# Seven products for the first column group too, one sum of weights added by DMA, and buffers granted by late times, in a two-layer encoder on one core

## The chip, the cores and the metric

The kernel runs on one core of a Trainium2 chip, as one program with one launch. The metric is the device time of one execution in microseconds. TensorE (PE) multiplies, VectorE (DVE) and ScalarE (ACT) prepare its operands and read its results, GpSimd (POOL) issues some transfers and does small work, SyncE (SP) issues the other transfers.

## The reference

The reference is a trunk of two layers on 512 tokens of width 1024, in float32. Each layer has a SwiGLU feed-forward, a mixer (layer 0: global and windowed attention; layer 1: neighbourhood attention), attention into 256 memory tokens, and a second SwiGLU feed-forward, each with a residual sum and a LayerNorm. The change is in the feed-forwards, of which there are four (0 to 3, each with its own weights):

```python
def swiglu(x, w_gate, w_up, w_down):            # 1024 -> 2816 -> 1024
    return (jax.nn.silu(x @ w_gate) * (x @ w_up)) @ w_down

y = swiglu(x, ffn_w_gate[i, 0], ffn_w_up[i, 0], ffn_w_down[i, 0])
x = layer_norm(ALPHA * x + 0.5 * y, ln_g[i, 0], ln_b[i, 0])
```

## The kernel before

**Numbers.** A float32 operand is split into a high part (a cast to fp32r, on ACT) and a low part (the difference, on DVE), and a product is three matmuls: high by high, high by low, low by high (`mm3`, line 334). `wide` (line 340) makes both parts of a weight tile of 128 x 1024 elements. For the tiles named in `ADDED` (only the fourth) the low part is made by a transfer that POOL issues and that adds the raw weights onto their negated high part in SBUF.

**The feed-forward** works on groups of 256 of the 2816 columns. `hidden` (line 585) computes gate and up of one group for all tokens. It cuts the work into quarters (the 1024 rows of the weights in two halves, gate and up as the other side; the tokens in two halves) and forms them from seven products of quarters with sums, in place of eight products. A product is 2 x 4 x 3 = 24 matmuls of 256 columns; `self.right[m]` is the tokens' side of product m, and `left[m]` the weights' side. The weights' side needs four sums, s1 to s4, each a DVE instruction over 128 x 1024 elements, then a high and a low part for each of seven tiles; s1 is up's first half plus up's second half, and s2 to s4 follow from it or from the raw weights:

```python
s1 = self.mix(new(), w["21"], w["22"], ALU.add)
s2 = self.mix(new(), s1, w["11"], ALU.subtract)
```

The tokens' side of products 5, 6, 7 and 4 (t1 to t4) is made by `mixed_features` (line 430) from the raw quarters of the features, once a feed-forward; products 1, 2 and 3 take plain quarters. The first group of each feed-forward does not use this: `ffn_by_tokens` (line 520) goes through the four tiles of 128 tokens and needs for each the features of this tile alone: 2 x 8 x 3 = 24 matmuls for gate and 24 for up, four times, so 192 matmuls of 256 columns, and then 8 transposes of 128 x 128 that turn the result back to the layout of `hidden`. `mixed_features` stands behind it. So a feed-forward is one group by tokens and ten by `hidden`, with the products into the output (`down_fast`, `down`) between them; the three groups at its end are those of `TAIL`.

**Between two stages** the LayerNorm goes by token tiles t = 0 to 3 (`finish`, line 727): DVE and ACT compute it, POOL raises one number a token to the power -0.5, then PE turns the tile to features (`to_features`, line 405: two times four transposes), ACT casts the high part (`xh`), DVE makes the low part (`xl`), and ACT copies the raw quarter for `mixed_features` (`keep`).

**The order of the work** is set by a planner, `Graph.emit` (line 178). Every operation is first recorded (all of them have line 153 in the profile, so tiles tell them apart). The planner then plays the program through with a cost for each operation: each engine takes, of what is ready, the operation that is earliest in program order, and the instructions are written out in that order, one in-order stream for each engine. An operation is ready when its operands are and when its tiles have a buffer. Buffers are shared by tag (35 of 4 KB a partition for `slab`, 5 PSUM banks for `u`, 3 for `d`), and are granted in the order in which the program asks for the tiles.

## Time and profile before

| | |
|---|---|
| median of 3 runs (lowest, highest) | 2147.81 us (2146.98, 2147.91) |
| the profiled execution: its time, its span | 2146.15 us, 2144.4 us |
| granted TensorE clock, mean | 0.999 of full speed |
| PE busy | 2123.5 us (99%), 14212 matmuls |
| weight loads (PEld) busy | 1959.1 us (91%) |
| DVE, ACT, POOL busy | 1701.1 us (79%), 1123.1 us (52%), 243.2 us (11%) |
| transfers | 261.41 MB, mean 122 GB/s |

The time is the device's for the whole execution; the span goes from the first to the last instruction, so the profiled execution has 1.75 us around its span. Of the table PE's row matters most: where PE is idle is where something else sets the time.

### The profile page before, as it was taken

The page shows a single profiled execution, that of the slowest core. Times are in us where ns is not written, and L with a number is a line of the kernel's source. Part 1 is how long each engine was busy: PE and PEld are TensorE (multiplying, and loading weights), DVE is VectorE, ACT ScalarE, POOL GpSimd, SP SyncE. Part 2 cuts the span into 40 slices and gives each one's busy share as a digit, 9 for nine tenths or more (in the row PEclk, how much of TensorE's full clock was granted, in tenths as well). Part 3 has the DMA queues.
Part 4 walks back from the last instruction along what each step waited for, and adds up shares of the span by engine and source line. Part 5 has one row for each costly group of instructions (what it writes and reads, how often), then busy time and mean ns, then how long its engine had stood idle before and what let it go on. Part 6 is the DMA issues. An engine that isn't in the chain of part 4 may idle for free.

```text
span 2144.4 us, 35357 instructions
## 1 busy us (share of the span) xinstructions
PE 2123.5 (99%) x14212; PEld 1959.1 (91%) x14212; DVE 1701.1 (79%) x2405; ACT 1123.1 (52%) x1722; POOL 243.2 (11%) x379
## 2 busy tenths in 40 slices
PE   9999999999999999999999999999999999999998
PEld 9989898778998898989999998999989989989897
DVE  7998976688855899889798989766678458998995
ACT  6555555467533564645464554545554435656452
POOL 0000004544000000000000000023320000000000
PEclk9999999999999999999999999999999999999999
DMA  7344358113433253435343525436455332434352
GB/s 207 99 138 129 118 148 208 20 40 89 151 103 112 89 157 109 129 108 148 108 116 111 148 89 158 148 84 162 134 185 154 99 109 79 129 108 137 102 152 62
DMA packets 186516, 261.41 MB, mean 122 GB/s; under 512 B 10864, under 2 KB 141552, under 8 KB 186352
## 3 DMA queue, kind: packets, MB, share of 16 engines
q1 hardware_dynamic: 175792, 221.40, 33.9%
q0 software_dynamic: 10560, 37.75, 8.3%
q8 instruction: 111, 1.82, 0.4%
q14 instruction: 53, 0.43, 0.1%
HBM read 217.17 MB, written 4.19 MB: 103 GB/s over the span
## 4 chain that ended last, share of the span: by engine, by line
PE 96%; DVE 1%; ACT 1%; issue 1%; POOL 0%; SPq 0%; DMA 0%; POOLq 0%; DVEq 0%; ACTq 0%
PE u L153 67%; PE d L153 29%; DVE slab L153 1%; ACT slab L153 0%; ACT t L153 0%; DVE x L153 0%; DVE mn L153 0%; DVE t L153 0%; ACT xh L153 0%; SPq L153 0%; ACT L153 0%; DMA slab<-t 0%; POOL slab L153 0%; POOL lny L153 0%; DVE l L153 0%
## 5 line engine op out<-in xcount | busy, mean ns | idle before, releaser
L153 DVE TENSOR_TENSOR slab<-slab,slab 128x1024 fp32r<-128x1024 f32 (+2 forms) x808 | 933.6, 1190 | 44.3 <-ACT slab L153 36.6
L153 ACT CAST slab<-slab 128x1024 fp32r<-128x1024 f32 (+1 forms) x620 | 608.6, 1016 | 194.1 <-DVE slab L153 155.1
L153 PE MATMUL u<-slab,slab 128*128 128x256 f32 (+2 forms) x4864 | 689.8, 300 | 1.4 <-ACT t L153 0.9
L153 PEld LDWEIGHTS u<-slab,slab 128*128 128x128 f32 x4864 | 644.4, 191 | 33.9 <-ACT t L153 1.6
L153 PE MATMUL u<-xh,slab 128*128 128x256 f32 (+2 forms) x3072 | 604.5, 294 | 0.0
L153 PE MATMUL d<-slab,slab 128*128 128x512 f32 (+2 forms) x2432 | 563.6, 384 | 3.8 <-DVE slab L153 3.0
L153 PEld LDWEIGHTS d<-slab,slab 128*128 128x128 f32 x2432 | 441.3, 188 | 88.8 <-DVE slab L153 5.4
L153 PEld LDWEIGHTS u<-xh,slab 128*128 128x128 f32 x3072 | 493.2, 192 | 12.1
L153 PE MATMUL u<-xl,slab 128*128 128x256 f32 (+2 forms) x1536 | 450.9, 294 | 0.0
L153 PEld LDWEIGHTS u<-xl,slab 128*128 128x128 f32 x1536 | 294.3, 192 | 5.9
L153 POOL DMA_DIRECT2D slab<-slab x52 | 45.1, 873 | 1079.1 <-ACT slab L153 576.8
L153 DVE SCALAR_TENSOR_TENSOR x<-d,x 128x512 f32<-128x512 f32 x184 | 126.1, 687 | 51.6 <-PE d L153 50.6
L153 DVE TENSOR_TENSOR t<-u,t 128x512 f32<-128x512 f32 (+1 forms) x128 | 88.1, 688 | 96.9 <-PE u L153 70.7
L153 ACT COPY t<-u 128x512 f32<-128x512 f32 x121 | 71.0, 587 | 136.3 <-PE u L153 136.3
L153 ACT CAST slab<-u 128x512 fp32r<-128x512 f32 (+3 forms) x161 | 77.5, 536 | 100.1 <-PE u L153 92.8
L153 DVE TENSOR_TENSOR slab<-u,slab 128x512 fp32r<-128x512 f32 (+3 forms) x161 | 91.7, 607 | 41.7 <-ACT slab L153 41.3
L153 PE MATMUL u<-slab,xh 128*128 128x256 f32 (+1 forms) x576 | 122.6, 308 | 1.7 <-ACT slab L153 1.4
L153 POOL TENSOR_TENSOR t<-t,l 128x256 f32<-128x256 f32 (+2 forms) x104 | 87.6, 857 | 275.9 <-DVE l L153 272.8
L153 ACT ACTIVATE t<-t 128x512 f32<-128x512 f32 x80 | 50.6, 633 | 128.1 <-DVE t L153 127.8
L153 PEld LDWEIGHTS u<-slab,xh 128*128 128x128 f32 x576 | 93.7, 191 | 7.9 <-ACT slab L153 1.9
L153 ACT CAST slab<-t 128x512 fp32r<-128x512 f32 x72 | 44.6, 619 | 92.5 <-DVE t L153 73.2
L153 PE MATMUL u<-slab,xl 128*128 128x256 f32 (+1 forms) x288 | 88.2, 308 | 0.0
(90 smaller groups left out, 1554.0 us busy)
## 6 DMA issues: line engine op xcount, KB each, us to landing
slab<-ffn_w_down SPq DMA_DIRECT2D x88, 512.0 KB
slab<-ffn_w_gate SPq DMA_DIRECT2D x86, 512.0 KB
slab<-ffn_w_up SPq DMA_DIRECT2D x86, 512.0 KB
slab<-slab POOLq DMA_DIRECT2D x52, 512.0 KB, 6.4
slab<-mem_w_kv SPq DMA_DIRECT2D x32, 512.0 KB
slab<-c_w_in SPq DMA_DIRECT2D x24, 512.0 KB
slab<-t SPq DMA_DIRECT2D x96, 128.0 KB
slab<-mem_w_q SPq DMA_DIRECT2D x16, 512.0 KB
```

The source lines that it names most:

```text
L153: op.call = lambda: fn(*args, **kw)
```

## The change

There are three edits.

1. In feed-forwards 1, 2 and 3 the first group is computed by `hidden` with seven products too; `ffn_by_tokens` is left for feed-forward 0. `mixed_features` is then called inside the first `hidden` (`early`), ahead of its products, and product 3, which needs plain quarters only, is put third, in a bank of its own (tag `d`). For the last token tile the high and low part of the first four feature blocks are no longer made from the transposes (`whole`), since t4 overwrites them.
2. In every `hidden` the sum s1 is no longer a DVE instruction: SP loads up's second half once more, into s1, and POOL then issues a transfer that adds up's first half from DRAM onto it. The raw halves are still loaded for the other sums.
3. The planner plays the program through up to four times (`PLANS`). After each pass `justify` works backwards and gives each operation the latest time at which it could begin, and the tiles of each tag then ask for buffers in the order of these times; the pass with the earliest end is written out.

```diff
+PLANS = 4
     def emit(self):
+        for n in range(PLANS):
+            got = self.plan()
+            if got is None:
+                break
+            if best is None or got[0] < best[0]:
+                best = got
+            self.justify()
+            for space in self.spaces.values():
+                space.queue.sort(key=lambda info: min((self.due[op] for op in info["users"]), default=0.0))
+    def justify(self):
+        last = max(self.begun.values()) + 5000.0
+        self.due, line = {}, {e: last for e in self.ENGINES}
+        for op in sorted(self.ops, key=lambda op: -self.begun[op]):
+            at = line[op.engine]
+            for u in op.users:
+                late = 0.0 if u.engine == op.engine and not op.dma else self.LATENCY[u.engine] + (165.0 if op.engine == "tensor" else 0.0)
+                late += 2600.0 + op.load if op.dma else 0.0
+                at = min(at, self.due[u] - late)
+            at -= op.ns
+            self.due[op] = line[op.engine] = at
...
-            self.split(ps.rearrange("p (k n) -> p k n", k=4), hi, lo)
+            if not self.keep or self.whole or q == 1 or t < 2:
+                self.split(ps.rearrange("p (k n) -> p k n", k=4), hi, lo)
...
-    def hidden(self, wg, wu, c0, dst):
+    def hidden(self, wg, wu, c0, dst, early=None):
-        s1 = self.mix(new(), w["21"], w["22"], ALU.add)
+        s1 = new()
+        for j, r in enumerate((512, 0)):
+            src = wu[r : r + 512, c0 : c0 + 256].rearrange("(k p) f -> p k f", p=P)
+            if j == 0:
+                nc.sync.dma_start(out=s1, in_=src)
+            else:
+                nc.gpsimd.dma_start(out=s1, in_=src, accum_op=ALU.add)
...
+        if early:
+            early()
...
         nc.scalar.activation(v, v, AF.Silu)
+        if early:
+            pd = self.ps("d")
+            product(3, pd, True)
         product(6, pa, False)
         nc.scalar.copy(u, pa)
+        if early:
+            self.mix(u, pd, u, ALU.add)
         product(5, pc, True)
         nc.scalar.copy(y, pc)
+        if early:
+            self.mix(u, pc, u, ALU.add)
...
             if n == 0:
-                self.ffn_by_tokens(wg, wu, i == 0, h1)
-                self.mixed_features()
+                if i == 0:
+                    self.ffn_by_tokens(wg, wu, True, h1)
+                    self.mixed_features()
+                else:
+                    self.hidden(wg, wu, c1, h1, self.mixed_features)
```

By instruction, the written program has on PE 72 fewer matmuls of 256 columns and 24 fewer transposes; on DVE 25 fewer instructions over 128 x 1024 elements (40 sums s1 go, 15 sums and low parts of the three new groups come); on SP and POOL 43 more transfers of 512 KB each from `ffn_w_up`, and on POOL 3 more that add the fourth tile's low part.

The order around the start of two of the three feed-forwards is shown now, in each engine's own rows. An `x_7_85` row turns the last token tile; `xh_80` and `xl_81` are the features' high and low parts; other numbers are tiles.

**Place 1: from feed-forward 1 to feed-forward 2, PE.** Before, PE turned the last token tile in the middle of the by-token products of the first tokens (banks `d_2059`, `u_2061`):

```order
L153 MATMUL d_2059<-slab_2056,xh_80 128x256
L153 MATMUL u_2043<-ident_75,x_7_85 128x128 x4
L153 MATMUL u_2044<-ident_75,x_7_85 128x128 x4
L153 MATMUL d_2059<-slab_2057,xh_80 128x256
L153 MATMUL d_2059<-slab_2056,xl_81 128x256
L153 MATMUL u_2061<-slab_2047,xh_80 128x256
L153 MATMUL u_2061<-slab_2048,xh_80 128x256
L153 MATMUL u_2061<-slab_2047,xl_81 128x256
```

Now it turns it after products 1 and 2 of the first group and four matmuls of the second group (`u_2104`). Then come matmuls of the second group's product 1 (`u_2103`), and, `d_2081`, product 3 of the first group, whose tokens' side needs `xh` of the tile just turned:

```order
L153 MATMUL u_2044<-ident_75,x_7_85 128x128 x4
L153 MATMUL u_2045<-ident_75,x_7_85 128x128 x4
L153 MATMUL u_2103<-xh_80,slab_2087 128x256
L153 MATMUL u_2103<-xl_81,slab_2087 128x256
L153 MATMUL u_2103<-xh_80,slab_2088 128x256
L153 MATMUL u_2103<-xh_80,slab_2087 128x256
L153 MATMUL u_2103<-xl_81,slab_2087 128x256
L153 MATMUL u_2103<-xh_80,slab_2088 128x256
L153 MATMUL u_2103<-xh_80,slab_2087 128x256
L153 MATMUL u_2103<-xl_81,slab_2087 128x256
L153 MATMUL u_2103<-xh_80,slab_2088 128x256
L153 MATMUL d_2081<-xh_80,slab_2063 128x256 x2
```

What moved: the first work that needs the last tile's features now stands 9 matmuls behind its transposes, where three token tiles' products stood before; from there the order goes on with 14 matmuls of `u_2103`, 22 of `d_2081` and then product 5 of the first group, which needs t1.

**Place 1, ACT.** Before, the high part of the last token tile came behind a cast of weights (`slab_2085`):

```order
L153 COPY slab_2034<-u_2033 128x4x128
L153 ACTIVATE t_1982_2060<-u_2058 128x256
L153 CAST slab_2085<-slab_2081 128x1024
L153 CAST xh_80<-u_2043 128x4x128
L153 CAST xh_80<-u_2044 128x4x128
L153 COPY slab_2032<-u_2043 128x4x128
L153 COPY slab_2034<-u_2044 128x4x128
L153 CAST slab_2088<-slab_2084 128x1024
L153 ACTIVATE t_1985_2063<-u_2061 128x256
L153 CAST slab_2076<-slab_2072 128x1024
```

Now the cast of the second group's s1 (`slab_2095<-slab_2089`, the tile that POOL's transfer completes) stands ahead of the copy of the last tile's first raw quarter (`slab_2033<-u_2044`) and of its `xh`:

```order
L153 COPY t_2000_2078<-u_2075 128x512
L153 CAST slab_2101<-slab_2085 128x1024
L153 CAST slab_2095<-slab_2089 128x1024
L153 COPY slab_2033<-u_2044 128x4x128
L153 CAST xh_80<-u_2045 128x4x128
L153 ACTIVATE t_2000_2078<-t_2000_2078 128x512
L153 ACTIVATE slab_2102<-slab_2085 128x1024
L153 CAST slab_2071<-slab_2067 128x1024
L153 COPY slab_2035<-u_2045 128x4x128
L153 CAST slab_2117<-slab_2113 128x1024
L153 CAST slab_2128<-slab_2112 128x1024
L153 CAST slab_2069<-slab_2068 128x1024
```

What moved: ACT, which takes its instructions in order, waits for that transfer before it serves the last token tile. SP issues the first half of this s1 behind the second of the twelve matmuls of the last token tile's last bank in feed-forward 1 (it takes over their buffer), and POOL's transfer follows when that has landed.

**Place 2: from the memory attention of layer 1 to feed-forward 3, ACT.** Before, the table load stood ahead of the last tile's `xh`, with the first of the activations by tokens:

```order
L153 COPY slab_3361<-u_3360 128x4x128
L153 ACTIVATE t_3289_3367,var_3366<-x_7_85,nmu_3365 128x1024
L153 ACT_TABLE_LOAD
L153 ACTIVATE t_3309_3387<-u_3385 128x256
L153 CAST slab_3412<-slab_3408 128x1024
L153 CAST slab_3415<-slab_3411 128x1024
L153 CAST xh_80<-u_3370 128x4x128
L153 CAST xh_80<-u_3371 128x4x128
L153 COPY slab_3359<-u_3370 128x4x128
L153 COPY slab_3361<-u_3371 128x4x128
```

Now the table load and the SiLU of the first group stand behind `xh` of the last tile, and the high part of t1 (`slab_3399<-slab_3395`) behind them:

```order
L153 ACTIVATE slab_3430<-slab_3413 128x1024
L153 COPY slab_3361<-u_3372 128x4x128
L153 CAST xh_80<-u_3373 128x4x128
L153 ACT_TABLE_LOAD
L153 ACTIVATE t_3328_3406<-t_3328_3406 128x512
L153 CAST slab_3399<-slab_3395 128x1024
L153 COPY slab_3363<-u_3373 128x4x128
L153 CAST slab_3423<-slab_3417 128x1024
L153 CAST slab_3397<-slab_3396 128x1024
L153 CAST slab_3401<-slab_3361 128x1024
L153 CAST slab_3442<-slab_3438 128x1024
```

What moved: the table load came into the chain from the last tile's transposes to t1. PE has between these transposes (`u_3372`, `u_3373`) and product 5 (`u_3405<-slab_3399`) 30 matmuls of 256 columns. The same pieces stand at the start of feed-forward 1, with 44 matmuls there, and with the cast of the second group's s1 between the SiLU and t1's high part. In all three places the tokens' sides of products 5, 6, 7 and 4 now follow the last tile's transposes at once, where they had the products of three token tiles ahead of them.

## Rows read from the trace of the kernel before

**Rows 1.** The page of the profile, its head: span, busy time of each engine.
```profile
span 2144.4 us, 35357 instructions
...
PE 2123.5 (99%) x14212; PEld 1959.1 (91%) x14212; DVE 1701.1 (79%) x2405; ACT 1123.1 (52%) x1722; POOL 243.2 (11%) x379
```

**Rows 2.** Waits of PE over the whole span: engine, tile, releaser; total us, times, longest.
```profile
PE d L153 <- DVE slab L153: 3.0, 4, 1.3
PE u L153 <- ACT t L153: 1.8, 2, 0.9
PE u L153 <- ACT slab L153: 1.4, 2, 1.2
...
PE u L153 <- POOL nhalf L153: 1.4, 1, 1.4
```

**Rows 3.** Stretches: the mixer of layer 0, then feed-forwards 1, 2 and 3.
```profile
core 0: us, PE busy (x) PEld busy (x) DVE busy (x) ACT busy (x) POOL busy (x), PEclk, DMA share, GB/s
351.00:564.00 213.00, 206.69 (x1104) 174.32 (x1103) 165.12 (x408) 126.01 (x283) 91.91 (x131) 1.00 0.31 81
752.00:1091.00 339.00, 338.88 (x2401) 319.74 (x2400) 295.92 (x340) 184.31 (x235) 12.53 (x17) 1.00 0.44 127
1091.00:1411.00 320.00, 319.95 (x2242) 300.78 (x2240) 280.93 (x324) 170.96 (x215) 16.46 (x21) 1.00 0.44 127
1823.00:2144.40 321.40, 312.16 (x2175) 292.94 (x2173) 271.49 (x313) 161.00 (x200) 11.60 (x16) 0.99 0.41 115
```

**Rows 4.** Chain that ended last, in order of time: start, us, what.
```profile
1091.15 61.35 PE u L153 x512
...
1163.41 10.88 PE u L153 x48
```

**Rows 5.** Groups on PE, shapes apart: xcount, busy us, mean ns.
```profile
L153 PE MATMUL u<-ident,t 128*128 128x128 f32 x440 | 57.9, 273 | 0.6 <-DVE slab L153 0.5
```

**Rows 6.** Groups on DVE, shapes apart.
```profile
L153 DVE TENSOR_TENSOR slab<-slab,slab 128x1024 fp32r<-128x1024 f32 x520 | 626.7, 1224 | 37.2 <-ACT slab L153 30.7 <-issue 3.3 <-ACT t L153 2.2
```

**Rows 7.** Groups on ACT, shapes apart.
```profile
L153 ACT CAST slab<-slab 128x1024 fp32r<-128x1024 f32 x572 | 581.8, 1049 | 165.3 <-DVE slab L153 126.3 <-PE d L153 28.5 <-PE u L153 7.1
...
L153 ACT ACTIVATE t<-t 128x512 f32<-128x512 f32 x80 | 50.6, 633 | 128.1 <-DVE t L153 127.8
...
L153 ACT CAST xh<-u 128x512 fp32r<-128x512 f32 x64 | 34.6, 590 | 71.8 <-PE u L153 71.4
...
L153 ACT COPY slab<-u 128x512 f32<-128x512 f32 x40 | 22.7, 589 | 4.8 <-DVE xl L153 2.7 <-PE u L153 2.0
...
L153 ACT ACT_TABLE_LOAD x6 | 7.7, 1283 | 3.2 <-DVE mn L153 2.4 <-PEq L1456 0.7
```

**Rows 8.** Groups on POOL, shapes apart.
```profile
L153 POOL DMA_DIRECT2D slab<-slab x52 | 45.1, 873 | 1079.1 <-ACT slab L153 576.8 <-PE u L153 259.1 <-DVE slab L153 107.6
```

**Rows 9.** DMA issues of the page: KB each, median us from issue to landing.
```profile
slab<-slab POOLq DMA_DIRECT2D x52, 512.0 KB, 6.4
...
slab<-ln_b POOLq DMA_DIRECT2D x8, 512.0 KB, 4.1
slab<-ln_g POOLq DMA_DIRECT2D x8, 512.0 KB, 7.1
```

**Rows 10.** Timeline of the start: the first load of x and its first use.
```profile
0.74 0.71 SPq L153 DMA_DIRECT2D x<-x  x1
...
5.22 0.60 PE L153 MATMUL u<-ident,x 128*128 128x128 f32 x4
```

**Rows 11.** Timeline of ACT at the start of feed-forward 3.
```profile
1802.13 1.15 ACT L153 ACTIVATE t<-x,nmu 128x1024 bf16<-128x1024 f32 x1
...
1803.39 1.28 ACT L153 ACT_TABLE_LOAD   x1
...
1807.06 1.08 ACT L153 CAST xh<-u 128x512 fp32r<-128x512 f32 x2
```

**Rows 12.** Timeline of PE at the end: its last instructions.
```profile
2119.82 15.35 PE L153 MATMUL d<-slab,slab 128*128 128x512 f32 x67
```

More of the change, by code (lines that the diff above doesn't have):

```diff
@@ L53, in __init__ @@
     def __init__(self, bufs):
-        self.free = [0.0] * bufs
-        self.queue = []
-        self.next = 0
+        self.bufs, self.queue = bufs, []
 class Recorder:
@@ L82, in __init__ @@
             setattr(self, e, Recorder(self, e))
+        self.gap = 40
         self.banks, self.after = None, None
@@ L179, in emit, with plan @@
         for info in self.tiles.values():
-            info["left"] = len(info["users"])
             for op in info["users"]:
                 op.frees.append(info)
+        for op in self.ops:
+            for d in op.deps:
+                d.users.append(op)
+        best = None
+        for n in range(PLANS):
[7 more added lines that the diff above has]
+                space.queue.sort(key=lambda info: min((self.due[op] for op in info["users"]), default=0.0))
+        self.end, self.stats = best
+        for _, _, op in self.stats:
+            self.tc.keep_in_program_order(op.call())
+    def justify(self):
[9 more added lines that the diff above has]
+            self.due[op] = line[op.engine] = at
+    def plan(self):
+        for info in self.tiles.values():
+            info["left"], info["at"] = len(info["users"]), 0.0
         now = {e: 0.0 for e in self.ENGINES}
@@ L188, in emit @@
             op.ready = 0.0
-            for d in op.deps:
-                d.users.append(op)
+        for space in self.spaces.values():
+            space.free, space.next = [0.0] * space.bufs, 0
         def release(op, t):
@@ L218, in emit @@
         done = 0
-        self.stats = []
+        stats, self.begun = [], {}
         line, span = {"sync": 0.0, "gpsimd": 0.0}, {"vector": (0.0, 0.0), "gpsimd": (0.0, 0.0)}
@@ L227, in emit @@
                     for at, r, _, _ in heapq.nsmallest(4, heaps[e]):
-                        if at < now[e] + op.ns * 0.6 and r < rank - 40:
+                        if at < now[e] + op.ns * 0.6 and r < rank - self.gap:
                             now[e] = at
@@ L239, in emit @@
                     best = (t, e)
-            assert best, "no instruction can start"
+            if best is None:
+                return None
             t, e = best
@@ L245, in emit @@
             _, _, op = heapq.heappop(ready[e])
-            self.tc.keep_in_program_order(op.call())
+            ns = op.ns
             other = {"vector": "gpsimd", "gpsimd": "vector"}.get(e)
@@ L250, in emit @@
                 if op.port == 2:
-                    op.ns += max(0.0, hi - t) if lo <= t else 0.0
+                    ns += max(0.0, hi - t) if lo <= t else 0.0
                 else:
-                    op.ns += max(0.0, min(t + op.ns, hi) - max(t, lo)) * (0.35 if e == "vector" else 0.7)
-                span[e] = t, t + op.ns
-            self.stats.append((e, t, op))
-            now[e] = t + op.ns
+                    ns += max(0.0, min(t + ns, hi) - max(t, lo)) * (0.35 if e == "vector" else 0.7)
+                span[e] = t, t + ns
+            stats.append((e, t, op))
+            self.begun[op] = t
+            now[e] = t + ns
             end = now[e] + (165.0 if e == "tensor" else 0.0)
@@ L271, in emit @@
                 info["left"] -= 1
-                info["at"] = max(info.get("at", 0.0), end)
+                info["at"] = max(info["at"], end)
                 if info["left"] == 0:
@@ L277, in emit @@
                 grant(space)
+        return max(now.values()), stats
 class Kernel:
@@ L292, in __init__ @@
         self.n = 0
-        self.keep = False
+        self.keep, self.whole = False, True
     def name(self, s):
@@ L544, in ffn_by_tokens @@
                 self.to_features(t)
+                self.whole = t < NT - 1
             both = []
@@ L621, in hidden @@
         nc.scalar.activation(v, v, AF.Silu)
+        if early:
+            pd = self.ps("d")
+            product(3, pd, True)
         product(6, pa, False)
         nc.scalar.copy(u, pa)
+        if early:
+            self.mix(u, pd, u, ALU.add)
         product(5, pc, True)
         nc.scalar.copy(y, pc)
+        if early:
+            self.mix(u, pc, u, ALU.add)
         product(7, pa, False)
         self.mix(y, pa, y, ALU.add)
-        product(3, pc, False)
-        self.mix(u, pc, u, ALU.add)
+        if not early:
+            product(3, pc, False)
+            self.mix(u, pc, u, ALU.add)
         nc.scalar.activation(u, u, AF.Silu)
```

## The prediction

> **What bounds the kernel now.** I read the head of the page first. PE is busy for 2123.5 of 2144.4 us [rows 1], so 20.9 us are all that better order could give, and whatever PE no longer has to do comes off the end. Next I looked where the 20.9 us lie, with the busy time by stretches. Feed-forwards 1 and 2 leave PE idle for 0.12 and 0.05 us (339.00 less 338.88, 320.00 less 319.95). Feed-forward 3 leaves 9.24 us (321.40 less 312.16), but that is the tail: PE's last matmuls end at 2135.17 us (2119.82 and 15.35) [rows 12], and the LayerNorm and the store of the last tile follow. The mixer of layer 0 leaves 6.31 us (213.00 less 206.69) [rows 3]. The list of PE's waits says the same from the other side: its longest entry is 3.0 us in four waits, and one of 1.4 us is the start's [rows 2]. The reader is to see that the three feed-forwards that are changed have no wait to remove, so there the gain can only be removed work, and every new wait is a loss. DVE is busy for 295.92 of 339.00 us there (87%), ACT for 184.31 (54%), and the transfers take 44% [rows 3]: DVE is near the bound, the others are not.
>
> **Edit 1, the work removed.** For each of three feed-forwards 192 matmuls become 168, and 8 transposes go. A stretch of 512 matmuls of 256 columns takes 61.35 us in the chain of work [rows 4], 0.1198 us each; 48 matmuls of 512 columns take 10.88 us, 0.2267 us each. The 440 transposes of `t` tiles take 57.9 us [rows 5], 0.1316 us each. So 3 x (24 x 0.1198 + 8 x 0.1316) = 3 x (2.88 + 1.05) = 11.8 us less for PE. This stands on PE's own chain, with nothing beside it to hide it.
>
> **Edit 1, the waits added.** What is new is the chain behind the last token tile: transposes, copy of the raw quarter, t1 on DVE, its high part on ACT, its low part on DVE, product 5; then t2 likewise, for product 6. Prices: ACT copy 0.589, ACT `xh` 0.590, table load 1.283, SiLU 0.633, weight-sized cast 1.049 [rows 7], DVE over 128 x 1024 elements 1.224 [rows 6]. I count from the end of the tile's first four transposes (the other four take PE 0.53).
>
> Feed-forward 3 (place 2): ACT does copy, `xh`, table load, SiLU, t1's high part, then DVE the low part: 0.59 + 0.59 + 1.28 + 0.63 + 1.05 + 1.22 = 5.36 us. DVE's t1 itself lies beside the table load. PE meanwhile has 0.53 + 30 x 0.12 = 4.13 us, and its first matmul of product 5 needs the high part alone (0.12 more): it waits 1.1 us. DVE makes t2 behind t1's low part (6.58); its high part ends at 7.63. PE would come to it after 11 further matmuls, at 4.13 + 1.32 + 1.1 = 6.55: 1.1 us more. Together 2.2 us.
>
> Feed-forward 1: the same with the cast of s1 in between, 6.41 us, against 0.53 + 44 x 0.12 + 0.12 = 5.93: 0.5 us. t2's high part ends at 6.41 + 1.22 + 1.05 = 8.68; PE comes to it at 5.81 + 15 x 0.12 + 0.5 = 8.11: 0.6 us more. Together 1.1 us.
>
> The cover for all this was the by-token products. In the trace the table load lay ahead of the last tile's `xh`, from 1803.39, and `xh` came only at 1807.06 [rows 11]; that cover is what the new order gives up.
>
> Feed-forward 2 (place 1) has no table load, but ACT waits for POOL's transfer of s1 ahead of the last tile's copy and `xh`. SP issues the first half when PE has 10 matmuls of 512 columns, 52 of 256 and 16 transposes to go to the end of the last tile's transposes: 2.27 + 6.23 + 2.11 = 10.6 us. How long this load takes no row says alone; the first piece of x is used 4.48 us after its issue (0.74 to 5.22) [rows 10], which I take. POOL's adding transfer takes 6.4 us to its landing as a median [rows 9] when its source is SBUF. So s1 lands 10.9 us after the issue. Then cast, copy and `xh`, 2.23 us: 13.1. PE needs `xh` nine matmuls (1.08 us) behind the transposes, at 11.7. It waits 1.4 us. Queued behind ACT's wait are the copy, `xh`, the SiLU and t1's high part; PE's 36 matmuls after that (4.3 us) cover the rest of t1's chain, as they cover it when ACT is not late.
>
> Here a rule speaks otherwise. By the Trainium skill, "DMA: Bandwidth & Descriptors", section "Anatomy of one DMA — SWDGE (gpsimd) path", a transfer issued by GpSimd takes about 2.0 us plus its bytes over 436 GB/s, an estimate of 3.2 us for 512 KB. By that rule s1 would land at 7.7, ACT would not wait and the sum below would be 1.4 us better. The trace differs: 52 adding transfers of this size take 6.4 us as a median [rows 9], and I stay with the row.
>
> **Edit 2.** DVE loses 25 instructions net, 25 x 1.22 = 31 us of 1701 [rows 1, 6]. DVE did not hold PE in the feed-forwards, so I cost this at nothing. 43 loads and 43 adding transfers come. The issue on POOL takes 0.87 us [rows 8], 38 us on an engine that is 11% busy [rows 1]. No row shows an adding transfer from DRAM with rows of 1 KB. From below, it lands as early as the plain load of `ln_b`, 4.1 us; from above, as late as `ln_g`, 7.1 us, and if issuing takes time by rows (512 in place of 128), 3 x 0.87 = 2.6 us more, 9.7 us [rows 8, 9]. I take 6.4 us, since only that row adds. With 4.5 us for the first half, s1 is there 10.9 us after SP's issue. Counting PE's work between the last matmul that frees s1's buffer and the last one ahead of its first use in ACT's or DVE's queue, as the order shows them, the place of feed-forward 2 is the shortest (6.2 us); all others but one (7.4) leave 8.6 us or more, over half of them 14 (and 5.8 or more from POOL's own turn). So ACT waits up to 2.3 us in a few groups. It is 54% busy there, and behind its wait usually stands a result of a product that PE only needs emptied one product (24 x 0.12 = 2.9 us) later. So the steady groups cost nothing if the landing is at 6.4; this cover is what a slow landing would use up.
>
> **Edit 3.** Where no tile is late a better order of grants brings nothing. In the mixer of layer 0 it could take some of 6.3 us or add to them; what is late next there is the same short ACT and DVE chains. I take nothing, with 2 us either way.
>
> **Sum.** -11.8 + 1.1 + 1.4 + 2.2 = -7.1 us. The profiled execution took 2146.15 us, which becomes 2139.1; the runs' median is 1.7 us above it, 2147.81, which becomes 2140.7 us.
>
> **The rivals.**
> *No new waits.* If loads land a microsecond earlier, if PE's work between is enough, and the table load falls in a gap, the whole 11.8 us are kept: 2136.0, and 2134 if the mixer gains too. For it: the order leaves PE other products to do in all three places, and the misses I worked out are 0.5 to 1.1 us at a time, the size of what such sums miss. Against: the table load, which must come somewhere between the memory attention's exponentials and the first SiLU. Chance 0.22.
> *Part of the gain is lost in the steady groups.* Landings vary, and where a transfer lands 2 to 3 us behind its median, ACT and then PE wait in perhaps a third of the groups for about half a microsecond: 14 x 0.5 = 7 us. That ends at 2147.7, no change that the measurement can tell (0.2%, or 4.3 us, is about what it can). Chance 0.15.
> *Slower: s1 is late in every group.* If the adding transfer from DRAM takes 9.7 us, s1 needs 14.2 us from SP's issue, and by the order 18 of the 43 groups leave less. The excess is up to 8 us of waiting on ACT, in order, with the results of products queued behind; PE hides some 2.9 us of each. 18 groups at 1 us for PE are 18 us: 2158.7. It decides from 11.4 us of such waits (7.1 + 4.3), so from a landing some 2.5 us later than I take. For it speaks the four times larger number of rows; against, that transfers of the same bytes by the same engine land in 4.1 to 7.1 us whatever they do [rows 9]. Chance 0.09.
> *The change not doing what it says* is excluded for the work: the written order has the 72 matmuls and 24 transposes fewer.
>
> **How the numbers follow.** My forecast has 0.54, "no new waits" 0.22, the steady loss 0.15, slower 0.09. Its own range is 2137 to 2144: each of three waits between nothing and twice its size. The range for all takes in the full gain with a little from the mixer (2135) and the steady loss (2147.7) and leaves out the slow case and the best of the mixer: 2135 to 2148. Faster by over 0.2% (below 2143.5) are "no new waits" and nearly all of the forecast's: 0.74. Within 0.2%: the steady loss and the forecast's edge, 0.17. Slower: 0.09.
>
> **What would show it.** PE's busy time falls to 2111.7, 14116 matmuls; anything else there makes the first term wrong. PE's waits gain entries for the features (`xh`) or t1 and t2 (a `slab` of ACT or DVE) at the start of feed-forwards 1 and 3 (near 740 and 1800) and one at feed-forward 2 (near 1070), each 0.5 to 2 us. Before these PE stays idle for nothing. A median landing of the new transfers over 9 us, or PE waits scattered over the ten groups of each feed-forward, would make the prediction wrong to the slow side; a feed-forward idle of 0.1 us as now, to the fast side.

## The result, and the profile after

| | before | after |
|---|---|---|
| median, in the runs made side by side (lowest, highest) | 2147.18 us (2146.3, 2147.91), 6 runs | 2157.7 us (2152.85, 2161.4), 6 runs |
| ratio, with its 95% interval | | 1.005 [1.004, 1.0059] |
| the profiled execution: time, span | 2146.15, 2144.4 us | 2155.86, 2154.1 us |

The change makes the kernel 10.5 us slower. The head of the page after:

```profile
span 2154.1 us, 35374 instructions
...
PE 2121.5 (98%) x14116; PEld 1952.4 (91%) x14116; DVE 1685.1 (78%) x2380; ACT 1135.0 (53%) x1725; POOL 308.7 (14%) x425
```

The work is gone as it should be (14116 matmuls, 96 fewer than in [rows 1]), yet the span is 9.7 us longer. So I read where PE waits, as in [rows 2]:

```profile
engine line waited for: us in total, times, longest us
PE d L153 <- ACT xh L153: 4.4, 1, 4.4
PE d L153 <- ACT slab L153: 4.0, 6, 2.2
PE u L153 <- ACT slab L153: 3.6, 7, 1.2
PE u L153 <- DVE slab L153: 3.6, 7, 0.6
PE u L153 <- ACT t L153: 3.4, 5, 1.0
```

One wait of 4.4 us stands out; the others are many and short. The same by stretches, as in [rows 3]: mixer of layer 0, feed-forwards 1, 2 and 3 between the same points of the program, and at the end two stretches of 4.8 us behind the long wait.

```profile
core 0: us, PE busy (x) PEld busy (x) DVE busy (x) ACT busy (x) POOL busy (x), PEclk, DMA share, GB/s
...
357.30:568.90 211.60, 206.65 (x1105) 174.57 (x1103) 166.41 (x408) 127.41 (x285) 89.06 (x127) 1.00 0.29 75
...
758.50:1102.50 344.00, 338.35 (x2369) 318.39 (x2368) 293.09 (x334) 187.12 (x236) 29.60 (x29) 0.99 0.60 158
1102.50:1420.30 317.80, 316.90 (x2210) 297.14 (x2209) 270.38 (x315) 169.24 (x210) 26.02 (x29) 1.00 0.56 156
...
1835.00:2154.10 319.10, 309.26 (x2143) 289.42 (x2141) 260.81 (x302) 154.88 (x192) 21.75 (x23) 0.99 0.52 139
1084.40:1089.20 4.80, 4.80 (x22) 4.80 (x23) 4.80 (x6) 4.70 (x6) 0.90 (x1) 0.50 0.60 154
1095.00:1099.80 4.80, 4.80 (x42) 4.80 (x41) 1.67 (x3) 3.58 (x6) 2.18 (x2) 1.00 0.44 63
```

The row that ends at 1102.5 holds the start of feed-forward 2. It lost 5.65 us of PE (0.12 before), and its clock is 0.99. The row of 4.8 us shows why: behind the wait PE was granted half its clock (0.50, the level of 1.2 GHz) and did 22 matmuls in a time in which it does 42 at full clock (the row under it), so 22 x 4.8 / 42 = 2.5 us of work took 4.8. The transfers' share rose from 0.44, 0.44 and 0.41 to 0.60, 0.56 and 0.52.

The place itself, from the timelines of ACT, SP, POOL and PE (start, us, what, and in brackets the idle time and what ended it):

```profile
1074.85 1.06 ACT L153 CAST slab<-slab 128x1024 fp32r<-128x1024 f32 x1
1082.29 1.04 ACT L153 CAST slab<-slab 128x1024 fp32r<-128x1024 f32 x1 [6.38 <-DMA slab<-ffn_w_up]
1083.24 0.58 ACT L153 COPY slab<-u 128x512 f32<-128x512 f32 x1
1083.72 0.59 ACT L153 CAST xh<-u 128x512 fp32r<-128x512 f32 x1
...
1068.36 2.28 SPq L153 DMA_DIRECT2D slab<-ffn_w_up  x3
1070.75 14.73 SPq L153 DMA_DIRECT2D slab<-ffn_w_gate  x2
...
1072.67 1.31 POOL L153 DMA_DIRECT2D slab<-ffn_w_up  x1 [3.47 <-PE u L153]
...
1084.37 0.80 PE L153 MATMUL d<-xh,slab 128*128 128x256 f32 x2 [4.43 <-ACT xh L153]
```

This is the chain that the prediction described: the cast of s1 stands ahead of the last tile's copy and `xh`, and waits for POOL's transfer, issued at 1072.67; the cast began at 1082.29, 9.6 us later. (POOL's row names PE as what ended its wait, at 1072.20. SP's half had landed 0.1 us before that, so either would have held it.) The first of SP's three transfers from 1068.36 on is s1's first half; the other two and the one at 1070.75 are quarters of the group after, and move at the same time. The landings of all transfers of this kind, as in [rows 9] (KB each, median us from issue to landing), and under them the same for two single ones, issued at 1190.48 and at 1111.28:

```profile
slab<-slab POOLq DMA_DIRECT2D x55, 512.0 KB, 7.1
slab<-ffn_w_up POOLq DMA_DIRECT2D x43, 512.0 KB, 9.3
...
slab<-ffn_w_up POOLq DMA_DIRECT2D x1, 512.0 KB, 10.9
...
slab<-ffn_w_up POOLq DMA_DIRECT2D x1, 512.0 KB, 5.8
```

The first of the two shares its time with five loads that SP issued around it and with adding transfers of POOL's; the second has neither beside it. I counted for each of the 43 the loads that SP issued from 3 us before POOL's issue to 1.5 us before the landing. The nine with none, and no other transfer of POOL's under way, take 5.8 to 7.1 us; of the 19 with three or more all but two take 9.3 us or more, up to 12.6. In 14 of these 19 another transfer of POOL's was under way at the issue as well; the five without one take 6.7 to 10.0 us. So both kinds of company go with a late landing, and the count doesn't tell their parts; it is also helped by the longer window of a transfer that lands late.

### The profile page after: what moved, and what is told of

The parts are those of the page before. It is cut to its first block, busy times and chain, and to the rows that moved or that the text cites. A ratio compares the mean times of both kernels' runs of the same rounds, so it can differ in the third digit from the quotient of the medians.

```text
span 2154.1 us, 35374 instructions
## 1 busy us (share of the span) xinstructions
PE 2121.5 (98%) x14116; PEld 1952.4 (91%) x14116; DVE 1685.1 (78%) x2380; ACT 1135.0 (53%) x1725; POOL 308.7 (14%) x425
## 3 DMA queue, kind: packets, MB, share of 16 engines
q1 hardware_dynamic: 198496, 243.95, 36.3%
## 5 line engine op out<-in xcount | busy, mean ns | idle before, releaser
L153 DVE TENSOR_TENSOR slab<-slab,slab 128x1024 fp32r<-128x1024 f32 (+2 forms) x783 | 908.6, 1194 | 92.1 <-ACT slab L153 56.2
L153 PE MATMUL u<-slab,slab 128*128 128x256 f32 (+2 forms) x5080 | 719.1, 299 | 7.0 <-DVE slab L153 2.9
L153 PEld LDWEIGHTS u<-slab,slab 128*128 128x128 f32 x5080 | 671.2, 191 | 42.1 <-DVE slab L153 4.1
L153 PE MATMUL u<-xh,slab 128*128 128x256 f32 (+2 forms) x3216 | 633.1, 294 | 1.3 <-ACT t L153 1.0
L153 PE MATMUL d<-slab,slab 128*128 128x512 f32 (+1 forms) x2432 | 565.0, 384 | 4.9 <-ACT slab L153 3.4
L153 PEld LDWEIGHTS u<-xh,slab 128*128 128x128 f32 x3216 | 517.2, 192 | 14.2 <-ACT t L153 1.2
L153 PE MATMUL u<-xl,slab 128*128 128x256 f32 (+2 forms) x1608 | 471.5, 293 | 0.0
L153 POOL DMA_DIRECT2D slab<-ffn_w_up x43 | 60.3, 1404 | 290.4 <-DMA slab<-ffn_w_up 174.2
L153 PE MATMUL u<-slab,xh 128*128 128x256 f32 (+1 forms) x384 | 87.4, 321 | 1.7 <-ACT slab L153 1.4
L153 PEld LDWEIGHTS u<-slab,xh 128*128 128x128 f32 x384 | 63.6, 190 | 7.8 <-ACT slab L153 2.0
```

The lines of the kernel that those rows point to most:

```text
L153: op.call = lambda: fn(*args, **kw)
```

## The experiments

### Each edit alone, and by twos

All run beside the kernel before (2146.8 and 2146.9 us as medians). Edit 2 undone is one line:

```diff
-s1 = new()
-for j, r in enumerate((512, 0)):
-    ...
+s1 = self.mix(new(), w["21"], w["22"], ALU.add)
```

Edit 3 undone is `PLANS = 1`; edit 1 undone puts the by-token branch of `ffn` back for all four feed-forwards, and `whole` is always true.

Edits 1 and 3, s1 on DVE: 

> The changed kernel with s1 added by DVE from the two quarters that are in SBUF anyway: edits 1 and 3 without edit 2. Theory A (the adding transfer from DRAM lands at 9.3 us in place of 6.4, and ACT's and DVE's in-order queues pass that on to PE): the waits for it go, PE keeps only the chain behind the last token tile (1.1 + 2.2 us), so 2147.2 - 11.8 + 3.3 = about 2139, and not above 2143. Rival B (the new first group and the new order of grants cost it, whatever s1 is made by): 2150 or more, with the long wait for xh at the start of feed-forward 2 still there.

Edit 2 alone: 

> The kernel before with edit 2 alone: s1 by the two transfers, grants in program order, the first groups by tokens. Theory A: the scattered waits of the changed kernel come without its gain. Its PE lost about 22 us more than before's; of these some 7 are at the start of feed-forward 2 and 3 belong to the chain behind the last tile, and neither exists here, so about 12 us more than before: 2159, anything from 2154 to 2165. Rival B: no change, 2145 to 2150. Rival C (it needs edit 2 together with the late-time grants): no change either.

Edit 1 alone: 

> The kernel before with edit 1 alone: the three first groups as seven products, s1 on DVE, grants in program order. Theory A: the 11.8 us of removed work less the chain behind the last tile, 2138 to 2141. Rival B: the start of feed-forward 2 shows PE waiting 4 us for xh and the kernel ends at 2147 or later.

Edit 3 alone: 

> The kernel before with edit 3 alone: buffers granted by late times, first groups by tokens, s1 on DVE. Theory D (edit 3 is what gives edit 1 its cover, by letting the second group's weights in early; by itself it has nothing to cover): within 3 us of before. Rival E (the late-time grants gain or lose by themselves, whatever the first groups are): 6 us or more to either side.

Edits 1 and 2: 

> The changed kernel with grants in program order: edits 1 and 2 without 3. Edit 1 alone came out at 2156.3, edit 2 alone at no change. Theory D (in program order s1 has room and edit 2 costs nothing; only the late-time grants bring it close to its use): 2156 within 3 us, with PE's three waits for xh of 2 to 3 us and the clock's three falls as in edit 1 alone. Rival A (the adding transfer is late wherever there is no by-token work ahead of it): 2160 or more.

Edits 2 and 3: 

> The changed kernel with the first groups by tokens: edits 2 and 3 without 1. Theory D: what edit 2 costs with late-time grants stays, without the 6.8 us at the start of feed-forward 2, so some 13 us above edit 3 alone: about 2158. Rival F (edit 2 costs only together with the new first groups): within 3 us of edit 3 alone.

| edits | median us | ratio to before, 95% interval |
|---|---|---|
| 1 | 2156.26 | 1.0046 [1.0034, 1.0059] |
| 2 | 2146.93 | 1.0002 [0.9993, 1.0011] |
| 3 | 2150.38 | 1.0016 [1.0007, 1.0025] |
| 1 and 2 | 2158.78 | 1.0058 [1.0045, 1.007] |
| 1 and 3 | 2137.97 | 0.9961 [0.9949, 0.9974] |
| 2 and 3 | 2169.5 | 1.0106 [1.0092, 1.012] |

With all three at 2157.7, edit 2 costs nothing alone (as a median; its eleven runs go from 2144.9 to 2152.5), 2.5 us on top of edit 1, which the two intervals don't tell from nothing, but 19.1 on top of edit 3 and 19.7 on top of 1 and 3. Edit 1 gains 12.4 us where edit 3 is there (2150.38 to 2137.97) and 11.8 where 2 and 3 are; without edit 3 it loses 9.4 or 11.9. So B, that the new groups cost it, fell for the whole change, and so did A in its plain form, that the sum by transfers costs wherever it is made. C and D were right in kind; D's sizes were not (edit 3 alone is 3.5 us off before, and edits 2 and 3 end 11 us above the 2158 expected).

Why edit 1 needs edit 3 is seen in edit 1 alone. Its PE at the start of feed-forward 1, and the three stretches behind such starts:

```profile
736.79 1.06 PE L153 MATMUL u<-ident,x 128*128 128x128 f32 x8 [1.19 <-DVE x L153]
740.47 0.58 PE L153 MATMUL d<-xh,slab 128*128 128x256 f32 x1 [2.62 <-ACT slab L153]
```

```profile
740.00:746.80 6.80, 6.11 (x27) 5.82 (x28) 6.70 (x7) 4.89 (x6) 0.00 (x0) 0.50 0.74 236
1081.40:1088.20 6.80, 6.08 (x27) 5.79 (x28) 6.80 (x7) 4.80 (x7) 0.00 (x0) 0.50 0.56 184
1818.60:1825.40 6.80, 6.19 (x30) 5.88 (x29) 6.70 (x6) 3.98 (x4) 0.00 (x0) 0.50 0.43 139
```

PE has run out of other products when it comes to the last tile and waits twice, and at each of the three starts half the clock follows. In the list of PE's waits of edit 1 alone these are the two longest entries:

```profile
PE d L153 <- ACT slab L153: 8.5, 5, 2.6
PE u L153 <- DVE x L153: 4.9, 5, 1.2
```

With late-time grants other products fill the gap: in edits 1 and 3 PE has 1.2 us of `u` matmuls between the last tile's transposes and the first `d` matmul at the start of feed-forward 1 (from 736.40 to 737.56). They have no entry for `x` of DVE, the one for `d` and ACT's `slab` is 1.3 us in all, and these are the longest:

```profile
PE u L153 <- ACT t L153: 2.7, 4, 0.8
PE u L153 <- ACT slab L153: 2.2, 3, 1.2
```

Edit 2's cost doesn't follow the time that ACT waits. The line of ACT's casts, for the whole change and then for edit 2 alone (busy, mean ns, idle before and what ended most of it):

```profile
L153 ACT CAST slab<-slab 128x1024 fp32r<-128x1024 f32 (+1 forms) x629 | 619.5, 1017 | 346.4 <-DVE slab L153 133.3 <-PE d L153 75.8 <-DMA slab<-ffn_w_up 74.9
```

```profile
L153 ACT CAST slab<-slab 128x1024 fp32r<-128x1024 f32 (+1 forms) x620 | 609.1, 1016 | 238.2 <-DVE slab L153 120.8 <-DMA slab<-ffn_w_up 74.7 <-PE d L153 24.1
```

74.9 us in one, 74.7 in the other. In the first 60.9 us of it, in 20 waits, ended with one of POOL's transfers and 14.0 with loads of SP's; in the second all of it ended with POOL's, in 13. So edit 2 alone makes ACT wait longer for s1, and its median pays nothing. The execution of it that was profiled is its slowest, though, 2152.46 us, and pays 6.3 us over before's. I take the rest of the difference to lie in what stands behind the wait and how soon PE wants it; no version shows that by itself.

Nor does it follow the median landing. The same row of POOL's transfers for edit 2 alone, and for edits 2 and 3:

```profile
slab<-ffn_w_up POOLq DMA_DIRECT2D x40, 512.0 KB, 7.2
slab<-ffn_w_up POOLq DMA_DIRECT2D x40, 512.0 KB, 7.7
```

The first pays nothing as a median and the second 19.1 us. Over 9 us land 9 of the 40 in the first, 15 in the second, and 22 of the 43 in the changed kernel.

### The planner told of the landing

```diff
+if "accum_op" in kw and ins[0].tensor.name not in self.tiles:
+    op.ns, op.lag = 1400.0, 4800.0
-end = line[e] + (2600.0 if e == "sync" else 1700.0)
+end = line[e] + (2600.0 if e == "sync" else 1700.0) + op.lag
```

`justify` reckons with `op.lag` too. 

> The changed kernel, whose planner now reckons with 1.40 us of issue and a landing 4.8 us later for the adding transfers from DRAM; what is computed and moved is the same. Theory A1 (the loss is that the order was written for a landing that the chip doesn't give): PE's waits shrink to a few us, 2140 to 2146. Rival A2 (the transfers themselves hold something: they queue behind each other or slow the other transfers, so that no order helps): 2152 to 2160, with ACT still waiting 50 us or more for slabs out of ffn_w_up.

2144.99 us, 0.999 [0.9982, 0.9999]: 12.7 us of the 19.7 come back with the same transfers, in another order. A1 holds for most of it. Told 7.5 us instead of 4.8: 

> As the version whose planner was told of a landing 4.8 us later (2145.0), now told 7.5 us, which is the slow end of the landings measured (11 to 12 us from the issue). If what is left there over the sum on DVE (7 us) is still lateness, in the crowded stretches: 2138 to 2142. If it is the transfers' load on the queues and on SBUF, which no order takes away: 2143 to 2148.

2150.49 us, 1.0018 [1.0009, 1.0027], outside both expectations. ACT no longer waits for s1 in any of its ten longest entries, but the new order waits elsewhere (PE on ACT for `slab`s: 10.4 us in 11 waits). A new order brings its own waits, so replanned versions can't say how much is s1's.

### The source, and one place

SBUF as the source of the second half, in rows of 4 KB: `nc.gpsimd.dma_start(out=s1, in_=w["21"], accum_op=ALU.add)`. 

> The changed kernel whose adding transfer takes its second half from the quarter that already lies in SBUF (rows of 4 KB) in place of DRAM (rows of 1 KB); the load of the first half stays. Theory G (the source makes it late: the many short rows from DRAM): landing like the other adding transfers, 6 to 7 us, issue 0.9 us, and 2139 to 2146. Rival H (a sum that comes by an adding transfer at all, behind a load, is too late for this order, whatever its source): 2150 to 2158.

2152.42 us, 1.0026 [1.0016, 1.0036]: H. At the start of feed-forward 2 that transfer took 9.5 us too, with SP's loads issued around it, ACT waited 6.16 us and PE 4.0. So 512 short rows are not needed to make it late there; I take the company to be what does. For the whole kernel the source does count: over all of POOL's 98 adding transfers the median is 6.7 us here and 13 take over 9 us, against 28 in the changed kernel, and the time is 5.3 us lower. (The planner wrote a new order for this version, so not all of the 5.3 us need be the source's.)

s1 on DVE in the three groups that follow the new first groups (`dve=n == 0 and i > 0`): 

> The changed kernel with s1 on DVE in three groups alone, the second of feed-forwards 1, 2 and 3; the other 40 sums stay transfers. If the wait for xh at the start of feed-forward 2 and the clock's fall behind it are due to that group's late s1, both go, 6.8 us, and the rest of edit 2's cost stays: about 2151. If the order there is tight for another reason, the wait stays and the time is 2155 to 2160.

2157.74 us, 1.006 [1.0047, 1.0074]. The wait and the fall of the clock at feed-forward 2 went (granted clock 1.00 from 1083 to 1090), but the new order had a wait of 4.9 us with half the clock behind it in feed-forward 0, at 283.9, and others later. The place moved, the cost stayed: a miss for the expected 2151.

### Waiting, load or order

The transfers made beside the sum on DVE, into a tile that nobody reads, with a slab fewer: 

> Edits 1 and 3 with s1 on DVE, and the 43 loads and 43 adding transfers of edit 2 made all the same, into a tile that nobody reads (one slab fewer, 34, to make room). Theory D (waiting for the sum is the cost): within 3 us of 2138. Rival A2 (the transfers cost by their load: they make other loads and sums late): 2145 or more, with PE's waits spread as in the changed kernel.

2171.65 us, 1.0109 [1.0095, 1.0123], and no answer. With nobody to wait for them the planner put these transfers early, and since all use one tile, SP stood still for 394.6 us behind them. The next versions therefore keep the changed kernel's order, instruction by instruction: the plan is made as before, and only what is issued is exchanged.

```diff
+ones = self.ident[:, None, :].to_broadcast([P, 8, P])
 s2 = self.mix(new(), s1, w["11"], ALU.subtract)
+nc.ops[-1].call = lambda: mine(out=flat8(s2), in0=ones, in1=flat8(w["11"]), op=ALU.subtract)
+...
+nc.ops[-2].call = lambda: nc.nc.scalar.copy(flat8(hi), ones)
+nc.ops[-1].call = lambda: mine(out=flat8(lo), in0=ones, in1=flat8(hi.bitcast(F32)), op=ALU.subtract)
```

> The changed kernel, every instruction in the changed kernel's order on every engine, all 86 transfers of s1 made; but the three readers of s1 (the cast of its high part, its low part, s2) read a constant tile of the same size in place of s1, so that nobody waits for it (s1 itself is left out of the result). Theory W (waiting for the late s1 is what costs): about what the sum on DVE gave, 2137 to 2141. Rival L (the transfers' load on queues and memory): 2152 or more, as the changed kernel. Rival O (the order itself, which the planner made for transfers, is worse whatever s1 does): 2145 or more here and in the version without transfers.

Without the transfers as well (their `call` issues nothing): 

> As the version in which nobody waits for s1, in the same order, and the 43 loads and 43 adding transfers of s1 are left out too. Theory W: the same as that version within 2 us. Rival L: 10 us or more below it. Rival O: both stay at 2145 or more.

With s1's readers as they were, and only POOL's transfers left out: 

> The changed kernel in the changed kernel's order, s1 read and waited for as there, but POOL's 43 adding transfers are left out, so that s1 holds its first half alone, loaded by SP. Theory W with the lateness in the adding step (9.3 us as a median): s1 is there some 9 us earlier and 2137 to 2143 comes out. If SP's load of the first half is already too late for this order: 2148 or more, with the wait for xh at the start of feed-forward 2 still over 2 us.

Medians: 2155.43 (1.0038 [1.0025, 1.005]), 2137.52 (0.9956 [0.9942, 0.9969]) and 2139.46 (0.9964 [0.9951, 0.9976]). The order is as good as that of edits 1 and 3 (2137.97), so O falls. SP's 43 loads and the waiting for them cost 2 us; POOL's step costs 18. The first of the three seemed to speak for load, but it still has this among ACT's waits (loads of SP's are in the line too):

```profile
ACT slab L153 <- DMA slab<-ffn_w_up: 26.7, 8, 7.5
```

Of PE's eight waits of 0.9 us or more behind the first 20 us, followed back through what each instruction waited for, five (0.9 to 2.3 us) come from a landing of s1, and two (1.75 and 2.6) from an older adding transfer that itself came behind one: the buffer of s1, which no reader holds, passes on at once, and its next owner waits. So that version had not taken the wait away. A tile of its own, with a control:

```diff
+self.unread = self.big.tile([P, 4, 256], F32, tag="unread", name="unread", bufs=1)
-t = pool.tile(shape, dtype, tag=tag, name=name, bufs=bufs)
+t = pool.tile(shape, dtype, tag=tag, name=name, bufs=min(bufs, 34))
```

> The changed kernel's order on every engine; the three readers of s1 read a constant tile, and the 43 loads and 43 adding transfers are made in their places in the order, but into one tile of their own that nobody reads and that takes no slab's place (34 slabs in place of 35), so that neither a reader nor a later owner of the buffer waits for them. (In the version in which nobody read s1, buffers of s1 passed to their next owners early, and those waited for the landing.) Theory W (waiting for the landing is the cost): 2137 to 2142. Rival L (the transfers' load makes the other transfers late): 2147 or more.

> The control for the version with a tile of its own: the same 34 slabs, the same readers of a constant, and no transfer of s1 at all. With 35 slabs that was 2137.5; if one slab fewer costs nothing in this order, the same within 2 us.

2183.9 and 2175.86 us (1.0169 and 1.0133): a slab fewer under an order made for 35 costs 38 us by itself, which hides the rest. The 8 us between the two are left open: with one tile for all of them SP stood still for 170.4 us behind these transfers. The last version needs no slab; its transfers go to DRAM (`nc.nc.gpsimd.dma_start(out=away, in_=src, accum_op=ALU.add)`, and SP's likewise). 

> The changed kernel's order on every engine with all 35 slabs; the three readers of s1 read a constant tile, and the 43 loads and 43 adding transfers are made in their places in the order with the same sources, but into 43 buffers of their own in DRAM, so that nothing waits for them, neither a reader nor a buffer's next owner (s1 is left out of the result). Without the transfers this was 2137.5. Theory W (waiting for the landing is the cost): 2137 to 2142. Rival L (the transfers make the other transfers late by their load): 2147 or more. Between the two lies a split: what is above 2137.5 is the load's part, at most, since DRAM is now written too.

2136.98 us, 0.9954 [0.994, 0.9967]. Its transfers by POOL, and its PE:

```profile
slab<-slab POOLq DMA_DIRECT2D x55, 512.0 KB, 7.5
...
away<-ffn_w_up POOLq DMA_DIRECT2D x43, 512.0 KB, 8.7
```

```profile
PE 2114.7 (99%) x14116; PEld 1949.2 (91%) x14116; DVE 1687.2 (79%) x2380; ACT 1135.6 (53%) x1725; POOL 300.8 (14%) x425
```

The same transfers in the same order, landing nearly as late (8.7 us), the other adding transfers later than in the changed kernel (7.5 us, 7.1 there), and the time is that of no transfers at all. So making the transfers costs nothing that can be measured here, and the 20 us are waiting for their landing. One thing is not in this version: that s1 is written into SBUF. Two rows speak against a cost of that. The queues of SP's loads (first line) and of POOL's transfers (second), with packets, MB and share of the 16 engines' time, for the changed kernel and then for this version:

```profile
q1 hardware_dynamic: 198496, 243.95, 36.3%
q0 software_dynamic: 33696, 61.87, 15.7%
```

```profile
q1 hardware_dynamic: 198496, 243.95, 36.2%
q0 software_dynamic: 33696, 61.87, 15.8%
```

The same 198496 packets of loads took the same time, within some 1%, beside transfers into SBUF and into DRAM. Nor did the engines work longer: DVE is busy for 1685.1 us in the changed kernel and 1687.2 here, ACT for 1135.0 and 1135.6. With that W is shown.

### More passes

Edits 1 and 3 with `PLANS = 12`: 

> Edits 1 and 3 with s1 on DVE (2138.0), and twelve passes of planning in place of four. If the order there is as good as the planner's model can tell, no change: 2136 to 2140. If later passes find room in the mixers: 2134 to 2136. A pass that looks better in the model and isn't on the chip: 2140 or more.

2138.22 us, 0.996 [0.9948, 0.9973]: no change from four passes. Edits 1 and 3 with s1 on DVE are the fastest version that leaves nothing of the result out, 8.8 us below the kernel before and 20 below the changed one.

## Why the prediction was wrong

**What held.** *The count*: PE's matmuls came out at 14116. *Bounds and mechanism*: DVE was no bound, and ACT in order behind s1 is where PE's longest wait came from. *The chain behind the last tile*, in the changed kernel: PE waited 0.5 us at the start of feed-forward 1 (predicted 1.1) and 1.6 at that of feed-forward 3 (2.2), 0.9 of it for the features' low part `xl`, which the sum did not have.

**What agrees by luck.** Without s1's part the sum was -11.8 + 1.1 + 2.2 = -8.5 us, and edits 1 and 3 measured 2146.78 - 2137.97 = 8.8. But there PE's busy time fell by 2123.5 - 2115.6 = 7.9 us, not 11.8, and of the 3.3 us of waits one of 0.7 came, at the start of feed-forward 1. So 3.9 us less work went than I had, and 2.6 us of waits stayed away, and the two nearly cancel. A small part of the first, 0.5 us, is the price of a transpose, 57.9 / 440 = 0.1316 us: from the start of one to the start of the next it is 0.109 as a median. Nor do the 12.4 and 11.8 us that edit 1 gains beside edit 3 confirm the 11.8: in the first a wait of 3.6 us in feed-forward 0 goes, which edit 1 doesn't touch, and PE's busy time falls by 10.0 and 10.9.

**The step that failed** is the price of edit 2: "I take 6.4 us, since only that row adds", and on it "the steady groups cost nothing if the landing is at 6.4". The landing was 9.3 us as a median, and from 5.8 to 12.6 one by one. At the start of feed-forward 2 this can be followed: I had 4.5 us for SP's half and 6.4 for POOL's, and a wait of 1.4; measured 4.3 (1068.36 to POOL's issue at 1072.67) and 9.6, and a wait of 4.4. The 3.0 us more of PE's wait are the 3.0 us more of the two landings. On top of that came what the sum did not have at all, the half clock behind the wait, 4.8 - 2.5 = 2.3 us. And "the steady groups cost nothing" fell: six more waits of PE (at 261.9, 263.2, 281.4, 1205.2, 2056.9 and 2058.1; 0.3 to 2.25 us, 5.2 in all), followed back through what each instruction waited for, come from a landing of s1. With the 4.4 these are 9.6 of PE's 23.3 us of waits.

The row was not wrong, its use was. A median over transfers that stand mostly alone on POOL's queue (44 of the 52 of before are issued with no other under way) was carried to transfers that don't (16 of 43), and that go out among SP's loads of a whole group. Nor was the median the row's spread: "4.1 to 7.1 us whatever they do" are medians of three kinds of transfer, and the 52 of before landed in 4.5 to 9.6 us one by one. With SBUF as a source 5.3 of the 20 us came back, in an order of its own, so the rows of 1 KB, which I had weighed, look like a part and not the whole. By the rule that I had cited (the Trainium skill, "DMA: Bandwidth & Descriptors", section "Anatomy of one DMA — SWDGE (gpsimd) path") it would have been 3.2 us, an estimate; no transfer of this kind landed under 5.8, so the trace disagrees with it even for those that stand alone.

**The slower rival was what happened.** It decided "from a landing some 2.5 us later than I take" and gave 2158.7; the landing was 2.9 later and the time 2157.7. Its shape was only roughly right. Comparing the start of PE's n-th instruction here and in edits 1 and 3: 4.0 us are lost in feed-forward 0, 6.8 at the start of feed-forward 2, and 8.8 in some twelve steps of 0.3 to 1.5 us, not 1 us in each of 18 groups. I gave it 0.09; that its condition was a landing at the upper bound of my own price should have weighed more. That the median met its condition is not the whole of it: edits 2 and 3 pay 19.1 us with a median of 7.7.

**Edit 3** at "nothing, with 2 us either way" was wrong as the price of an edit by itself (it loses 3.5 us alone, with one wait of 3.6 us in feed-forward 0) and, more so, in company: it makes edit 1 gain 12 us where it lost 9, and turns edit 2 from nothing into 19. My waits were counted in the changed order, so the first was in the sum without my knowing it. The second I argue only: granting a buffer at the latest time leaves no slack for a transfer that is later than the planner thinks, and the planner thinks 4.5 us for one that takes 9.3. The 12.7 us that came back with a truer landing fit this; that 7.5 us in place of 4.8 gave 5.5 of them away again does not by itself.

**DVE's work** fell by 1727.9 - 1685.1 = 43 us by edit 2, 1.0 us for each of 43 sums, and it bought nothing, as predicted.

Open: of the 19.0 us between the spans with and without edit 2, 13.7 are PE's waits (23.3 us in all against 9.6) and 2.3 the half clock at feed-forward 2. The other 3 us lie in short pieces that I did not follow.

## What to carry to other kernels

Price a transfer by its landing in the company that it will have: look at the spread of the nearest row and at what else is in flight, not at the median alone. An engine's instruction that is taken over by a transfer is a gain only if the engine was the bound; here DVE was not, and a cheap, certain 1.0 us was traded for a landing after 6 to 12 us ahead of an engine that takes its work in order. Edits to an order depend on each other: edit 2 costs nothing as a median alone and 19 to 20 us beside edit 3. And when a new plan takes one wait away, look for it elsewhere.

## What was not expected of the hardware

An adding transfer of 512 KB from DRAM in rows of 1 KB, 5.8 us to landing alone and up to 12.6 among SP's loads and other adding transfers, is dear in its issue too. It takes 1.40 us on POOL, against 0.89 for one out of SBUF:

```profile
L153 POOL DMA_DIRECT2D slab<-ffn_w_up x43 | 60.3, 1404 | 290.4 <-DMA slab<-ffn_w_up 174.2 <-DVE slab L153 66.2 <-DVE t L153 25.3
L153 POOL DMA_DIRECT2D slab<-slab x55 | 48.7, 886 | 815.4 <-ACT slab L153 423.1 <-DVE slab L153 293.3 <-PE d L153 58.5
```

PE's clock was granted at half behind waits of PE: for 6.8 us each behind the three starts of feed-forwards in edit 1 alone, where PE had waited 1.2 and then 2.2 to 2.6 us, and behind the 4.4 us in the changed kernel. With its 2.3 us of lost clock that wait cost 6.7 us.

And 45 MB of added transfers (308.08 MB with DRAM as their end, against 262.98 without them in the same order) cost no measurable time when nothing waited for them.
